# TensorE's parts of the S5 set-up behind later elementwise parts, small loads on GpSimd's queue, a first block split at 256 columns

## The chip, the core and the metric

The kernel runs on one core of one Trainium2 chip. The core's engines run side by side and each takes its own instructions strictly in the order in which they stand: TensorE (PE in the profile, its weight loads PEld), VectorE (DVE), ScalarE (ACT), GpSimd (POOL) and SyncE (SP), which here only starts DMA transfers. Sixteen DMA engines move the data. The metric is the device time of one launch in microseconds; lower is better.

## The reference

One layer of a hybrid decoder. 2064 prompt rows (16 meta tokens and 2048 tokens) and 8 running sequences of 4 tokens each pass through it, with a model width of 1024, all in float32:

```python
hn = rms_norm(x, lp['norm_mix_pre'])
proj = hn @ lp['w_in']                                  # 1024 x 4616
u, qkv, z, a, bt, gates = jnp.split(proj, [o1, o2, o3, o4, o5], axis=-1)
y_s5, h_re_n, h_im_n = s5_mix(u, ...)                   # 32 groups of a diagonal complex state, 64 states each
qkv_c, conv_new = short_conv(qkv, conv_buf, lp['gdn_conv_w'])      # 4 taps, then silu
g = -jnp.exp(gdn_A_log) * jax.nn.softplus(a + gdn_dt_bias)         # decay rates
beta = jax.nn.sigmoid(bt)
o, S = gdn_segment(q, k, v, g, beta, S)                 # gated delta rule, chunks of 64
mix = (sigmoid(ga) * br_a + sigmoid(gb) * br_b) @ lp['w_out']
x = x + rms_norm(mix, lp['norm_mix_post'])
x = x + rms_norm((silu(f @ w_ffn_gate) * (f @ w_ffn_up)) @ w_ffn_down, lp['norm_ffn_post'])
```

The S5 part needs tables that depend on the parameters alone: for each group the powers of a complex number `a_bar`, and matrices of 128 columns made of these powers with B and C.

## The kernel before, in words

The kernel works in phases: `p1` (the projection of the normalised input with `w_in`, the convolution, the S5 and the delta-rule work beside it), `merge`, `way_out`, `gate_up` and `down`. The change lies in `p1`, roughly the first 1300 of the 3287 us.

**The main stream.** A matrix product of float32 accuracy is three products of rounded parts (`mm3`, lines 161 to 163: high x high, high x low, low x high). The weight of 128 output columns (`wload`) comes by one DMA into `wr` (two buffers), is rounded by ACT into `wh`, and its remainder is split off in halves by POOL and DVE into `wl` (lines 146, 148, 149; three buffers each). The tokens come in blocks of 512 columns; block 0 has 560, since the 16 meta tokens and 32 sample tokens are with it. `p1_features` loads tiles of 128 tokens (`xt`, four buffers), squares them on ACT, makes the reciprocal root by a chain of a dozen small DVE operations, scales, transposes on PE (line 263), and writes `pgh` (ACT, line 268) and `pgl` (DVE, line 269). A pass takes two blocks with each unit of weights: 12 units of q, k, v (`psq`), 20 of gates (`psg`), 4 of u (`psu`). A product of more than 512 columns is cut in two by `colgroups`: 280 and 280.

**The side work.** After each half product of 8 k-steps `proj` calls `tick`, which advances four queues of generators by fractions of a step. `qf` holds the features of the next block, `qa` the delta rule's decays and triangular inverses, `qb` the S5 set-up and later the S5 groups, `qc` the delta-rule chunks. Each `yield` in a generator ends a step. `s5_setup` is such a generator; in its last part it handles the 32 groups in sets of four, and each set has five steps: V (POOL multiplies twice, DVE subtracts, line 1064, one DMA); K (PE multiplies V, line 1075, ACT copies, eight DMAs); V2 (line 1066); W (line 1062); and Wo (PE transposes W, line 1097, ACT copies, one DMA).

**What sets the order.** The instructions of an engine are not in the order of the code: the framework builds the whole program and then places each instruction by priority and by its own estimate of when operands are ready. So the order on each engine is fixed before the run, and an instruction that is late holds up all that stand behind it. Buffers come from pools: all of `ut`, `raw`, `cy`, `ct`, `gt`, V, V2, W and their helpers share one pool of eleven (`c2`).

**Small loads.** `gains` (lines 195 to 208) loads two gain vectors, the convolution's taps `cw` and the decay rates' constants `alog` and `dtb`, and computes `nea` from `alog` with `exp`, 15 small DVE operations. `pads` (338, 341) writes zeros to 20 places of two scratch tensors. All of them go by SP, as do the tokens and the weights.

Of the kernel before, what the change touches and what calls it, by code (L numbers as in the profile page):

```python
# [7 lines left out]
F32 = mybir.dt.float32  # L8
# [62 lines left out]
class Trunk:  # L71
# [118 lines left out]
    def gains(self):  # L190
        nc, c = self.nc, self.p1c
        def col(name, n):
            t = self.const.tile([P, n], F32, name="c_" + name)
            a = self.io[name]
            nc.sync.dma_start(t, ap_of(a, 0, [[1, P], [P, n]]))
            return t
# [4 lines left out]
        nc.sync.dma_start(self.cw, ap_of(self.io["gdn_conv_w"], 0, [[1, P], [1536, 4], [P, 12]]))  # L201
        self.alog = c.tile([P, H], F32, name="alog")
        nc.sync.dma_start(self.alog, ap_of(self.io["gdn_A_log"], 0, [[0, P], [1, H]]))
        self.dtb = c.tile([P, H], F32, name="dtb")
        nc.sync.dma_start(self.dtb, ap_of(self.io["gdn_dt_bias"], 0, [[0, P], [1, H]]))
        self.nea = c.tile([P, H], F32, name="nea")
        self.exp(self.nea, self.alog, "h")
        nc.vector.tensor_scalar(self.nea, self.nea, -1.0, None, op0=OP.mult)
# [103 lines left out]
    def p1_setup(self):  # L312
# [6 lines left out]
        for i in range(3):  # L319
            st = self.c2("stc")[:24, :512]  # L320
            nc.sync.dma_start(st, io["state_conv"].rearrange("o b j w -> (o b j) w")[:, 512 * i:512 * i + 512])
            sts.append(st)
# [10 lines left out]
    def pads(self):  # L333

        nc, z = self.nc, self.zero
        for m in range(4):
            for s, c in ((4, NL), (0, NL + 8)):
                nc.sync.dma_start(self.u_d[P * m:P * m + P, s:s + 4, c:c + 8],
                                  z[:, 0:32].rearrange("p (s n) -> p s n", s=4))
        for m in range(12):  # L340
            nc.sync.dma_start(ap_of(self.qkv_d, m * P * QW + NM, [[QW, P], [1, 16]]), z[:, 0:16])
# [4 lines left out]
    def p1_u(self, b, m, xh, xl, w):  # L346
# [5 lines left out]
        for c0, c1 in self.colgroups(width):  # L352
# [14 lines left out]
    def p1_qkv(self, b, m, xh, xl, w_):  # L367
# [10 lines left out]
        for c0, c1 in self.colgroups(width):  # L378
# [36 lines left out]
    def gdn_setup(self):  # L415
# [26 lines left out]
        nc.sync.dma_start(raw, self.wcols(self.w_in, C_AB, 8))  # L442
# [17 lines left out]
    def p1_ab(self, b, xh, xl):  # L460
# [3 lines left out]
        for c0, c1 in self.colgroups(width):  # L464
# [10 lines left out]
    def gdn_ab(self, b, ab):  # L475
# [43 lines left out]
        v.tensor_scalar(self.beta[:, sl], xa, 0.5, 0.5, op0=OP.mult, op1=OP.add)  # L519
        yield  # L520
# [363 lines left out]
    def s5_setup(self):  # L884
# [126 lines left out]
        for hf in range(2):  # L1011
# [37 lines left out]
            yield  # L1049
            for g0 in range(h0, h0 + 16, 4):  # L1050
# [20 lines left out]
                yield  # L1071

# [15 lines left out]
                V2 = f4(self.c2("V2"), 8)  # L1088
                outer(V2, (CR, CI), (R2, R1), "n", 1, 9)
                nc.sync.dma_start(self.wv_d[gs, :, 3].rearrange("g p (t c) -> p g t c", c=16), V2)  # L1090
                yield
                W = f4(self.c2("W"), 8)
                outer(W, (BR, BI), (W1, W2), "+", 0, 8)
                yield
                ps = self.pt.tile([P, BLK], F32, tag="pt", name="pst")
                for i in range(4):
                    nc.tensor.transpose(ps[:, P * i:P * i + P], W[:, i].rearrange("p t c -> p (t c)"), self.ident)
                Wo = self.tm.tile([P, D], F32, tag="tm", name="s5w").rearrange("p (g k m) -> p g k m", g=4, k=2)
                p4 = ps.rearrange("p (g m) -> p g m", g=4)
                nc.scalar.activation(Wo[:, :, 0], p4, AF.Copy)  # L1100
                nc.scalar.activation(Wo[:, :, 1, 0:64], p4[:, :, 64:P], AF.Copy)
                nc.scalar.activation(Wo[:, :, 1, 64:P], p4[:, :, 0:64], AF.Copy, scale=-1.0)
                nc.sync.dma_start(self.wv_d[gs, :, 0:2].rearrange("g p k m -> p g k m"), Wo)
                yield
# [105 lines left out]
    def p1_gate(self, b, m, xh, xl, w):  # L1210
# [5 lines left out]
        for c0, c1 in self.colgroups(width):  # L1216
# [731 lines left out]
```

## Time and profile before

| | us |
|---|---|
| median of 3 runs | 3285.52 (3281.97 to 3293.22) |
| the profiled execution | 3288.82 |
| its span in the profile | 3287.0 |
| PE busy in the span | 3105.4 (94%) |
| DVE busy in the span | 2015.5 (61%) |
| PE busy from 160 to 440 us | 249.34 of 280 |
| DVE busy from 160 to 440 us | 242.12 of 280 |

A row of the profile names the line of the kernel, the engine, the operation and the tile that it writes and reads. An engine with q behind its name (SPq) is its sequencer starting a DMA. The waits list says which engine waited for which line of another, how long in total, how often, and the longest time. PEclk is the share of its full clock that TensorE was granted.

### The profile page before, as it was taken

Reading aid. Unit: us, or ns where it says so; the run is one execution under the profiler, and the core shown is the slowest. Engines: PE = TensorE matmul, PEld = TensorE weight load, DVE = VectorE, ACT = ScalarE, POOL = GpSimd, SP = SyncE. Lnnn points to the kernel's source line nnn. Section 1 sums busy time; section 2 is a strip of 40 time slices with the busy share of each in tenths; the row PEclk is TensorE's granted clock in tenths of the full one; section 3 lists DMA queues with packets and bytes.
Section 4 is the critical chain, followed back from the end, with each engine's and each line's share of the span. In section 5 each row is a group of like instructions: output and inputs, shape, how many; then the busy total and the mean of one; then the engine's idle time right before and its main releaser. Section 6 shows DMA issues by size and latency. Waiting matters only on the chain. (4 is left out here: it accounts for less than half of the span.)

```text
span 3287.0 us, 47621 instructions
## 1 busy us (share of the span) xinstructions
PE 3105.4 (94%) x17461; PEld 2709.1 (82%) x17461; DVE 2015.5 (61%) x4648; ACT 1120.6 (34%) x1944; POOL 910.1 (28%) x903
## 2 busy tenths in 40 slices
PE   6998999999999999999999699999999999999998
PEld 5887778877777777988777699999999998887776
DVE  6888854657897546553444766676676664246235
ACT  4633222433232224221233444444444444223211
POOL 1123441123332212201111344434434444122110
PEclk9999999999999999999999799999999999999999
DMA  5336456545465435653553433333333334235224
GB/s 118 123 101 178 123 156 182 123 122 149 140 190 168 126 110 156 189 158 119 176 180 127 154 104 104 103 121 104 103 103 107 103 103 134 92 102 141 82 59 69
DMA packets 469018, 419.30 MB, mean 128 GB/s; under 512 B 120794, under 2 KB 393370, under 8 KB 468784
## 3 DMA queue, kind: packets, MB, share of 16 engines
q1 hardware_dynamic: 458576, 382.18, 39.9%
q0 software_dynamic: 10208, 34.09, 3.7%
q8 instruction: 137, 2.24, 0.3%
q14 instruction: 97, 0.79, 0.1%
HBM read 288.27 MB, written 127.65 MB: 127 GB/s over the span
## 5 line engine op out<-in xcount | busy, mean ns | idle before, releaser
L161 PE MATMUL psf<-xh,ah 128*128 128x348 f32 (+1 forms) x1848 | 598.8, 324 | 31.9 <-ACT sn L1534 20.2
L163 PE MATMUL psf<-xh,al 128*128 128x348 f32 (+1 forms) x1848 | 593.2, 321 | 6.8 <-DVE al L1476 6.8
L162 PE MATMUL psf<-xl,ah 128*128 128x348 f32 (+1 forms) x1848 | 593.0, 321 | 0.0
L161 PEld LDWEIGHTS psf<-xh,ah 128*128 128x128 f32 x1848 | 348.1, 188 | 41.5 <-ACT sn L1534 29.0
L163 PEld LDWEIGHTS psf<-xh,al 128*128 128x128 f32 x1848 | 347.6, 188 | 7.1 <-DVE al L1476 7.1
L162 PEld LDWEIGHTS psf<-xl,ah 128*128 128x128 f32 x1848 | 348.1, 188 | 0.0
L161 PE MATMUL psg<-pgh,wh 128*128 128x512 f32 (+1 forms) x800 | 300.0, 375 | 1.3 <-ACT wh L146 1.3
L1638 PE MATMUL psr<-wu,hh 128*128 128x512 f32 (+2 forms) x748 | 295.4, 395 | 4.2 <-POOL wu L148 4.2
L163 PE MATMUL psg<-pgh,wl 128*128 128x512 f32 (+1 forms) x800 | 291.4, 365 | 6.0 <-DVE wl L149 5.2
L1637 PE MATMUL psr<-wu,hh 128*128 128x512 f32 (+2 forms) x748 | 294.3, 395 | 0.0
L162 PE MATMUL psg<-pgl,wh 128*128 128x512 f32 (+1 forms) x800 | 291.3, 364 | 0.0
L1640 PE MATMUL psr<-wu,hl 128*128 128x512 f32 x704 | 277.6, 395 | 0.0
L148 POOL TENSOR_TENSOR wl<-wr,wh 128x512 fp32r<-128x512 f32 x92 | 143.8, 1563 | 389.5 <-ACT wh L146 318.9
L161 PE MATMUL psq<-pgh,wh 128*128 128x512 f32 (+1 forms) x480 | 180.4, 376 | 0.3 <-ACT pgh L268 0.3
L163 PEld LDWEIGHTS psg<-pgh,wl 128*128 128x128 f32 x800 | 155.5, 195 | 30.3 <-DVE wl L149 5.4
L1476 POOL TENSOR_TENSOR al<-R,ah 128x1024 fp32r<-128x1024 f32 x62 | 162.8, 2626 | 50.4 <-ACT ah L1475 50.4
L161 PEld LDWEIGHTS psg<-pgh,wh 128*128 128x128 f32 x800 | 156.0, 195 | 23.7 <-issue 2.9
L162 PEld LDWEIGHTS psg<-pgl,wh 128*128 128x128 f32 x800 | 155.9, 195 | 22.0 <-issue 2.5
L1638 PEld LDWEIGHTS psr<-wu,hh 128*128 128x128 f32 (+2 forms) x748 | 137.7, 184 | 42.9 <-POOL wu L148 6.7
L163 PE MATMUL psq<-pgh,wl 128*128 128x512 f32 (+1 forms) x480 | 172.9, 360 | 0.0
L162 PE MATMUL psq<-pgl,wh 128*128 128x512 f32 (+1 forms) x480 | 172.6, 360 | 0.0
L1637 PEld LDWEIGHTS psr<-wu,hh 128*128 128x128 f32 (+2 forms) x748 | 137.6, 184 | 35.9
(497 smaller groups left out, 6733.9 us busy)
## 6 DMA issues: line engine op xcount, KB each, us to landing
wr<-w_in SPq DMA_DIRECT2D x72, 512.0 KB
araw<-w_ffn_gate SPq DMA_DIRECT2D x31, 1024.0 KB
araw<-w_ffn_up SPq DMA_DIRECT2D x31, 1024.0 KB
wr<-w_ffn_down SPq DMA_DIRECT2D x44, 512.0 KB
zg_d<-gt SPq DMA_DIRECT2D x80, 256.0 KB
h_d<-hm SPq DMA_DIRECT2D x44, 348.0 KB
qkv_d<-cy SPq DMA_DIRECT2D x48, 256.0 KB
hr<-h_d SPq DMA_DIRECT2D x16, 768.0 KB
```

The costliest lines, as they stand in the source:

```text
L148: nc.gpsimd.tensor_sub(lo[:, :c], raw[:, :c], hi[:, :c].bitcast(F32))
L161: t.matmul(ps, wh, xh, start=first, stop=False, **kw)
L162: t.matmul(ps, wh, xl, start=False, stop=False, **kw)
L163: t.matmul(ps, wl, xh, start=False, stop=last, **kw)
L1476: eng.tensor_sub(flat(lo), x, flat(hi).bitcast(F32))
L1637: nc.tensor.matmul(ps, hi[:, k, cl], wh[:, cs], start=k == 0, stop=False)
L1638: nc.tensor.matmul(ps, hi[:, k, cl], wl[:, cs], start=False, stop=both and k == n - 1)
L1640: nc.tensor.matmul(ps, lo[:, k, c - c0:c - c0 + r], wh[:, cs], start=False, stop=k == n - 1)
```

## The change

- `gains`, `p1_setup`, `pads` and `gdn_setup` start their small loads and zero writes with `nc.gpsimd` and no longer with `nc.sync`.
- `alog`, `dtb` and `nea` move from `gains` to `gdn_setup`.
- `p1` cuts the 560 columns of block 0 at 256 (256 and 304) and no longer at 280; the other phases keep `colgroups`.
- `gdn_ab` has one more `yield` before the matmuls that sum up the decays.
- In `s5_setup` a set of four groups has four steps: V; V2; W; K. The transposes and copies of W (`late`) run at the start of the V2 step of the following set, and once more at the end of a half.

```diff
@@ gains
             a = self.io[name]
-            nc.sync.dma_start(t, ap_of(a, 0, [[1, P], [P, n]]))
+            nc.gpsimd.dma_start(t, ap_of(a, 0, [[1, P], [P, n]]))
             return t
         self.g_ffn = col("norm_ffn_pre", 8)
         self.g_gdn = col("gdn_norm", 1)
         nc.vector.tensor_scalar(self.g_gdn, self.g_gdn, 0.5, None, op0=OP.mult)
         self.cw = c.tile([P, 4, 12], F32, name="cw")
-        nc.sync.dma_start(self.cw, ap_of(self.io["gdn_conv_w"], 0, [[1, P], [1536, 4], [P, 12]]))
-        self.alog = c.tile([P, H], F32, name="alog")
-        nc.sync.dma_start(self.alog, ap_of(self.io["gdn_A_log"], 0, [[0, P], [1, H]]))
-        self.dtb = c.tile([P, H], F32, name="dtb")
-        nc.sync.dma_start(self.dtb, ap_of(self.io["gdn_dt_bias"], 0, [[0, P], [1, H]]))
-        self.nea = c.tile([P, H], F32, name="nea")
-        self.exp(self.nea, self.alog, "h")
-        nc.vector.tensor_scalar(self.nea, self.nea, -1.0, None, op0=OP.mult)
+        nc.gpsimd.dma_start(self.cw, ap_of(self.io["gdn_conv_w"], 0, [[1, P], [1536, 4], [P, 12]]))

@@ p1_setup
             st = self.c2("stc")[:24, :512]
-            nc.sync.dma_start(st, io["state_conv"].rearrange("o b j w -> (o b j) w")[:, 512 * i:512 * i + 512])
+            nc.gpsimd.dma_start(st, io["state_conv"].rearrange("o b j w -> (o b j) w")[:, 512 * i:512 * i + 512])
             sts.append(st)
@@ pads, p1_cols
             for s, c in ((4, NL), (0, NL + 8)):
-                nc.sync.dma_start(self.u_d[P * m:P * m + P, s:s + 4, c:c + 8],
+                nc.gpsimd.dma_start(self.u_d[P * m:P * m + P, s:s + 4, c:c + 8],
                                   z[:, 0:32].rearrange("p (s n) -> p s n", s=4))
         for m in range(12):
-            nc.sync.dma_start(ap_of(self.qkv_d, m * P * QW + NM, [[QW, P], [1, 16]]), z[:, 0:16])
+            nc.gpsimd.dma_start(ap_of(self.qkv_d, m * P * QW + NM, [[QW, P], [1, 16]]), z[:, 0:16])
+
+    def p1_cols(self, width):
+        return [(0, 256), (256, width)] if width > BLK else [(0, width)]

@@ p1_u
-        for c0, c1 in self.colgroups(width):
+        for c0, c1 in self.p1_cols(width):
             ps = self.pm.tile([P, BLK], F32, tag="pm", name="psu")[:, :c1 - c0]
@@ p1_qkv
-        for c0, c1 in self.colgroups(width):
+        for c0, c1 in self.p1_cols(width):
             ps = self.pm.tile([P, BLK], F32, tag="pm", name="psq")[:, :c1 - c0]
@@ gdn_setup
         self.abw = c.tile([P, 8, 2, 8], F32R, name="abw")
-        nc.sync.dma_start(raw, self.wcols(self.w_in, C_AB, 8))
+        nc.gpsimd.dma_start(raw, self.wcols(self.w_in, C_AB, 8))
+        self.alog = c.tile([P, H], F32, name="alog")
+        nc.gpsimd.dma_start(self.alog, ap_of(self.io["gdn_A_log"], 0, [[0, P], [1, H]]))
+        self.dtb = c.tile([P, H], F32, name="dtb")
+        nc.gpsimd.dma_start(self.dtb, ap_of(self.io["gdn_dt_bias"], 0, [[0, P], [1, H]]))
+        self.nea = c.tile([P, H], F32, name="nea")
+        self.exp(self.nea, self.alog, "h")
+        nc.vector.tensor_scalar(self.nea, self.nea, -1.0, None, op0=OP.mult)
         r = raw.rearrange("p a b -> p (a b)")
@@ gdn_ab
-        for c0, c1 in self.colgroups(width):
+        for c0, c1 in self.p1_cols(width):
             ps = self.pm.tile([P, BLK], F32, tag="pm", name="psa")[:16, :c1 - c0]
@@ gdn_ab
         v.tensor_scalar(self.beta[:, sl], xa, 0.5, 0.5, op0=OP.mult, op1=OP.add)
+        yield
         yield
@@ s5_setup
             yield
+            late = None
             for g0 in range(h0, h0 + 16, 4):
@@ s5_setup
                 yield
+                if late:
+                    late()
+                V2 = f4(self.c2("V2"), 8)
+                outer(V2, (CR, CI), (R2, R1), "n", 1, 9)
+                nc.sync.dma_start(self.wv_d[gs, :, 3].rearrange("g p (t c) -> p g t c", c=16), V2)
+                yield
+                W = f4(self.c2("W"), 8)
+                outer(W, (BR, BI), (W1, W2), "+", 0, 8)
+                yield

@@ s5_setup
                 yield
-                V2 = f4(self.c2("V2"), 8)
-                outer(V2, (CR, CI), (R2, R1), "n", 1, 9)
-                nc.sync.dma_start(self.wv_d[gs, :, 3].rearrange("g p (t c) -> p g t c", c=16), V2)
-                yield
-                W = f4(self.c2("W"), 8)
-                outer(W, (BR, BI), (W1, W2), "+", 0, 8)
-                yield
-                ps = self.pt.tile([P, BLK], F32, tag="pt", name="pst")
-                for i in range(4):
-                    nc.tensor.transpose(ps[:, P * i:P * i + P], W[:, i].rearrange("p t c -> p (t c)"), self.ident)
-                Wo = self.tm.tile([P, D], F32, tag="tm", name="s5w").rearrange("p (g k m) -> p g k m", g=4, k=2)
-                p4 = ps.rearrange("p (g m) -> p g m", g=4)
-                nc.scalar.activation(Wo[:, :, 0], p4, AF.Copy)
-                nc.scalar.activation(Wo[:, :, 1, 0:64], p4[:, :, 64:P], AF.Copy)
-                nc.scalar.activation(Wo[:, :, 1, 64:P], p4[:, :, 0:64], AF.Copy, scale=-1.0)
-                nc.sync.dma_start(self.wv_d[gs, :, 0:2].rearrange("g p k m -> p g k m"), Wo)
-                yield
+
+                def late(gs=gs, W=W):
+                    ps = self.pt.tile([P, BLK], F32, tag="pt", name="pst")
+                    for i in range(4):
+                        nc.tensor.transpose(ps[:, P * i:P * i + P], W[:, i].rearrange("p t c -> p (t c)"), self.ident)
+                    Wo = self.tm.tile([P, D], F32, tag="tm", name="s5w").rearrange("p (g k m) -> p g k m", g=4, k=2)
+                    p4 = ps.rearrange("p (g m) -> p g m", g=4)
+                    nc.scalar.activation(Wo[:, :, 0], p4, AF.Copy)
+                    nc.scalar.activation(Wo[:, :, 1, 0:64], p4[:, :, 64:P], AF.Copy)
+                    nc.scalar.activation(Wo[:, :, 1, 64:P], p4[:, :, 0:64], AF.Copy, scale=-1.0)
+                    nc.sync.dma_start(self.wv_d[gs, :, 0:2].rearrange("g p k m -> p g k m"), Wo)
+            yield
+            late()
+            yield

@@ p1_gate
-        for c0, c1 in self.colgroups(width):
+        for c0, c1 in self.p1_cols(width):
             ps = self.pm.tile([P, BLK], F32, tag="pm", name="psg")[:, :c1 - c0]
```

**GpSimd's queue at the start.** `c_norm_ffn_pre`, `c_gdn_norm`, `cw`, `abr`, `alog` and `dtb` are small loads; `u_d` and `qkv_d` are the scratch tensors that get zeros; a shape such as 128x48x1 means 48 single elements in each of 128 partitions. Before:

```order
L172 IOTA jp 128x128
L422 IOTA ii 64x64
L423 IOTA ip 64x1
L452 MEMSET U 128x512
L452 MEMSET T_756 64x256
L148 TENSOR_TENSOR wl<-wr,wh 128x512 x2
L1078 MEMSET s5k 16x4x128
```

After:

```order
L172 IOTA jp 128x128
L195 DMA c_norm_ffn_pre<-norm_ffn_pre 128x8x1
L195 DMA c_gdn_norm<-gdn_norm 128x1
L201 DMA cw<-gdn_conv_w 128x48x1
...
L438 DMA abr<-w_in 128x8x8
L440 DMA alog<-gdn_A_log 128x4
L148 TENSOR_TENSOR wl<-wr,wh 128x512
L442 DMA dtb<-gdn_dt_bias 128x4
...
L331 DMA u_d<-zero 128x4x8 x7
L148 TENSOR_TENSOR wl<-wr,wh 128x512
L331 DMA u_d<-zero 128x4x8
L334 DMA qkv_d<-zero 128x16 x12
L148 TENSOR_TENSOR wl<-wr,wh 128x512
```

The first, second and third POOL half of `wl` now stand behind 5, 13 and 26 DMAs; before, none stood there.

**SP's queue at the start**, the tokens `xt` and the weights `wr`. Before, from the third row of tokens on:

```order
L223 DMA xt<-x_prompt 128x1024 x2
L195 DMA c_norm_ffn_pre<-norm_ffn_pre 128x8x1
...
L144 DMA wr<-w_in 128x8x128
...
L223 DMA xt<-x_prompt 16x1024
L225 DMA xt<-x_sample 32x1024
L228 DMA xt<-x_prompt 128x1024
...
L228 DMA xt<-x_prompt 128x1024 x2
...
L228 DMA xt<-x_prompt 128x1024
...
L144 DMA wr<-w_in 128x8x128 x3
```

After:

```order
L216 DMA xt<-x_prompt 128x1024 x2
L144 DMA wr<-w_in 128x8x128 x3
L216 DMA xt<-x_prompt 16x1024
L218 DMA xt<-x_sample 32x1024
L221 DMA xt<-x_prompt 128x1024
L144 DMA wr<-w_in 128x8x128
L221 DMA xt<-x_prompt 128x1024 x3
```

The fifth weight load now stands ahead of three of block 1's four token tiles; with two buffers of `wr` it can start only when the third `wl` is split. Before, the third to fifth stood behind all the tokens.

**The S5 set-up on GpSimd**, from the first set's V on (`ow` is the second product of a pair). Before:

```order
L1059 TENSOR_TENSOR V<-s5c,s5r 128x576
L148 TENSOR_TENSOR wl<-wr,wh 128x512
L1060 TENSOR_TENSOR ow<-s5c,s5r 128x576
L1083 TENSOR_TENSOR s5k<-s5k,dg 16x4x16
L1059 TENSOR_TENSOR V_3038<-s5c,s5r 128x512
L1060 TENSOR_TENSOR ow<-s5c,s5r 128x512
L1081 TENSOR_TENSOR dg<-ident,s5a 16x64
L148 TENSOR_TENSOR wl<-wr,wh 128x512
L1059 TENSOR_TENSOR W<-s5bb,s5rr 128x512
```

After:

```order
L1064 TENSOR_TENSOR V<-s5c,s5r 128x576
L148 TENSOR_TENSOR wl<-wr,wh 128x512
L1065 TENSOR_TENSOR ow<-s5c,s5r 128x576
L1064 TENSOR_TENSOR V_2959<-s5c,s5r 128x512
L1065 TENSOR_TENSOR ow<-s5c,s5r 128x512
L148 TENSOR_TENSOR wl<-wr,wh 128x512
L1064 TENSOR_TENSOR W<-s5bb,s5rr 128x512
L1065 TENSOR_TENSOR ow<-s5bb,s5rr 128x512
L1097 TENSOR_TENSOR s5k<-s5k,dg 16x4x16
```

K's addition (`s5k`), which waits for PE and ACT, stood between V and V2 and now stands behind W.

## The prediction

> **What bounds the kernel now.** I read the page's busy shares first, then the slices, the windows of the stage that the change touches, and the list of waits in it.
>
> ```profile
> PE 3105.4 (94%) x17461; PEld 2709.1 (82%) x17461; DVE 2015.5 (61%) x4648; ACT 1120.6 (34%) x1944; POOL 910.1 (28%) x903
> PE   6998999999999999999999699999999999999998
> DVE  6888854657897546553444766676676664246235
> 160.00:440.00 280.00, 249.34 (x1471) 220.83 (x1470) 242.12 (x852) 89.40 (x164) 102.62 (x118) 0.93 0.48 133
> 267.00:270.40 3.40, 3.40 (x11) 2.83 (x12) 2.95 (x18) 1.15 (x3) 0.00 (x0) 0.50 0.66 180
> 852.00:862.00 10.00, 7.28 (x27) 5.45 (x26) 8.93 (x43) 3.39 (x7) 0.63 (x2) 0.83 0.39 115
> ```
>
> In a row of the windows stand the stretch, its length, then PE, PEld, DVE, ACT and POOL busy, the granted clock, the DMA share and GB/s. TensorE bounds the whole (94%), so a microsecond is won only where TensorE stands still or runs slowly. The S5 set-up lies in 160 to 440 us, where TensorE idles 280 − 249.3 = 30.7 us and was granted 0.93 of its clock: 280 × 0.07 = 19.6 us more. The clock falls behind a standstill: TensorE waited 4.75 us before 266.9, and the next 3.4 us went at 0.50. But VectorE is busy for 242.1 of these 280 us: it is the next bound there, 37.9 us behind. TensorE's waits, for 160 to 440 us and in the last row for the whole run (total, times, longest):
>
> ```profile
> PE pst L1097 <- DVE W L1062: 12.5, 3, 4.8
> PE psg L163 <- DVE wl L149: 5.2, 1, 5.2
> PE pst L1075 <- DVE V L1064: 4.7, 1, 4.7
> PE pst L525 <- DVE k_gg L517: 3.2, 2, 1.9
> PE pst L1047 <- DMA ctl<-s_C_re: 3.0, 1, 3.0
> ...
> PE pst L525 <- DVE k_gg L517: 5.9, 3, 2.7
> ```
>
> **Part 1: W and V later on TensorE, one more step before the decays' sums.** One of the three waits for W, as the timeline of all engines has it:
>
> ```profile
> 260.83 2.31 DVE L395 SCALAR_TENSOR_TENSOR cy<-raw,cw,cy 128x512 f32<-128x512 f32 x3
> 263.27 1.11 POOL L1059 TENSOR_TENSOR W<-s5bb,s5rr 128x512 f32<-128x512 f32 x1 [3.46 <-DVE cy L395]
> 266.14 0.69 DVE L1062 TENSOR_TENSOR W<-W,ow 128x512 f32<-128x512 f32 x1
> 266.89 1.08 PE L1097 MATMUL pst<-ident,W 128*128 128x128 f32 x4 [4.75 <-DVE W L1062]
> ```
>
> POOL stood for 3.46 us until VectorE was through with the convolution, so W came late, and TensorE with its whole stream behind the four transposes. In the new order 24 products and four transposes more stand between W's first product and its transposes. How much time is that? The distance between two products comes from their starts:
>
> ```profile
> 119.83 0.29 PE L161 MATMUL psq<-pgh,wh 128*128 128x280 f32 x1
> ...
> 123.21 0.29 PE L163 MATMUL psq<-pgh,wl 128*128 128x280 f32 x1
> 123.62 0.40 PE L162 MATMUL psq<-pgl,wh 128*128 128x512 f32 x1
> ...
> 128.73 0.40 PE L163 MATMUL psq<-pgh,wl 128*128 128x512 f32 x1
> 46.31 0.60 PE L263 MATMUL pst<-ident,xt 128*128 128x128 f32 x4
> ```
>
> 3.38 us over 26 steps is 0.130 us for 280 columns; 5.11 over 22 is 0.232 for 512; a transpose takes about 0.11 (0.60 for four, less the pipeline's tail). So W's transposes stand 12 × 0.232 + 12 × 0.120 + 4 × 0.11 = 4.7 us later, about the longest wait (4.8), and W's POOL part moves up by one weight half. K's product of V comes two steps later still. The sums that need `k_gg` move by 23 × 0.232 = 5.3 us against a longest wait of 2.7. All three kinds can vanish: 12.5 + 4.7 + 3.2 = 20.4 of the 30.7 us in this stage. Their share of the lost clock is 20.4/30.7 × 19.6 = 13.0, so 33.4 us if nothing else becomes late.
>
> Something else does become late, since VectorE cannot do its 242.1 us in less. Its own waits there:
>
> ```profile
> DVE V L1064 <- POOL ow L1060: 14.6, 3, 5.8
> DVE wl L149 <- ACT wh L146: 5.8, 6, 2.8
> ```
>
> Of its 37.9 idle us the 14.6 for POOL's product of V are not touched: V, `ow` and a weight half stand on POOL in the same succession as before. That leaves 37.9 − 14.6 = 23.3 as the most that the stage can shrink. TensorE's wait of 5.2 for `wl` is one for VectorE too, and a stage that runs faster brings it nearer: the late thing after W and V is `wl`. I leave it standing and take 23.3 − 5.2 = **−18**, between 0 (VectorE hands every microsecond over to `wl`) and −23.3. V and W also hold their buffers of the pool of eleven a step or two longer; the price is inside these ends.
>
> The third wait for `k_gg` lies at 853 us, outside the stage: 2.7 us and 10 × 0.17 = 1.7 of clock. VectorE is busy for 8.93 of the 10 us there, so of 4.4 I take **−2** (0 to −4.4).
>
> **Part 2: small loads by GpSimd.** No row shows such loads on POOL, so their price is bounded from POOL's other DMAs (mean ns of one behind the busy time):
>
> ```profile
> L287 POOL DMA_DIRECT2D f_d<-fo x36 | 26.0, 722 | 165.9 <-ACT fo L286 161.5 <-issue 4.3
> L1405 POOL DMA_DIRECT2D y_prompt<-xr x16 | 8.9, 554 | 11.1 <-DVE xr L1404 11.1
> L1654 POOL DMA_DIRECT2D y_prompt<-facc x16 | 13.8, 859 | 79.5 <-DVE facc L1651 79.5
> ```
>
> One of 128 rows takes 0.554 us, one with two pieces in each partition (256) 0.722: 0.55 each, and 0.168 for every further 128 pieces. By this `c_norm` (8 x 128 pieces) takes 1.7, `c_gdn` 0.55, `cw` (48 x 128) 8.4: 11.8 with the 1.1 us of constants ahead. `abr` (8 x 128) and `alog` make 14.1, and the first weight half (1.27) ends at 15.4. Then `dtb`, seven `u_d` of 4 x 128 (1.05 each) and the second half: 24.6; one `u_d`, twelve `qkv_d` and the third half: 33.5.
>
> What waits for that is SP. The fourth weight load needs the second half, and the last 48 tokens of block 0 stand behind it; the fifth needs the third, and three tiles of block 1 stand behind it. Before, they went like this (SP), and TensorE's starts answer to them:
>
> ```profile
> 8.72 5.65 SPq L203 DMA_DIRECT2D alog<-gdn_A_log  x1
> ...
> 19.85 0.44 SPq L223 DMA_DIRECT2D xt<-x_prompt  x1
> ...
> 28.51 0.84 SPq L228 DMA_DIRECT2D xt<-x_prompt  x2
> ...
> 36.45 0.33 SPq L228 DMA_DIRECT2D xt<-x_prompt  x1
> 10.64 1.27 POOL L148 TENSOR_TENSOR wl<-wr,wh 128x512 fp32r<-128x512 f32 x1 [8.63 <-ACT wh L146]
> 24.59 0.60 PE L161 MATMUL psq<-pgh,wh 128*128 128x280 f32 x1
> 52.74 2.11 PE L263 MATMUL pst<-ident,xt 128*128 128x128 f32 x8 [5.58 <-DVE xt L252]
> ```
>
> SP loses the 5.65 us for which `alog` was stuck behind `cw`, and products of 256 columns need only the first two token tiles, so the first product can come before 24.59. But it lacks the tail at once: the 48 tokens go out at 24.6 and not at 19.85 (4.7 later), block 1's second tile at 34 and not at 28.5 (5.5 later), its last one earlier than 36.45. TensorE's total work here is the same, so what counts is when block 1 can run on. I take **+3**, between 0 and 5.5, since the last tile gains. Its ends: −5.6 if each DMA costs 0.55 whatever its pieces (1.1 + 26 × 0.55 + 3 × 1.27: the third half can be through at 19, and the 5.58 us wait ahead of 52.74 goes). If instead each further 128 pieces cost a whole DMA (0.55), the 85 further ones ahead of the third half cost 85 × (0.554 − 0.168) = 32.8 us more: +36. The row of 859 ns is between: 26 × 0.305 = 7.9 more, +11.
>
> A rule of the Trainium skill bears on these ends: DMA: Bandwidth & Descriptors, "Anatomy of one DMA — SWDGE (gpsimd) path", says that many descriptors can be emitted before their number is felt; by it the start gains 5.6, while the rows above show a step of 0.168 at 256 pieces already. Against the change speaks SBUF — State Buffer, "SBUF: two separate sides": a DMA of GpSimd's queue cannot have its descriptors written while VectorE runs in a mode that takes both ports. The 859 beside 554 ns for the same shape would fit; by it the start is +11.
>
> **Part 3: 256 and 304.** 0.232/512 × 560 columns is 0.254, and twice 0.130 is 0.260: the two halves cost by column, so the cut is free. Bound: if 256 costs no less than 280, 36 units x 24 products x 0.0106 us = +9.2.
>
> **The sum** on the profiled execution's 3288.8 us (span 3287.0): −18 − 2 + 3 = −17, so 3271.8. That execution lies 3.3 above the median of 3285.5, so **3269** on the median. Between 440 and 500 us, behind the stage, what is won is kept, since TensorE does not wait at all:
>
> ```profile
> 440.00:500.00 60.00, 60.00 (x358) 48.41 (x357) 25.33 (x59) 11.99 (x30) 22.76 (x25) 0.94 0.64 177
> ```
>
> **Rivals.** (a) Slower: POOL's DMAs go by pieces. One place decides, the three weight halves behind `cw` (48 x 128 pieces), `abr` and the zeros on POOL. If a further 128 pieces cost 0.55 us, the start is +36 against −20 in the two other terms: 3285.5 + 16 = 3301.5. It turns to a loss from 85 × (p − 0.168) = 17, that is p = 0.37 us. For it: pieces of 4 bytes have no row here. Against it: the step of 0.168 is less than half of that. Chance 0.17. (b) The same: VectorE takes the waits over. The transposes no longer wait, but `wl`, 242.1 of 280 us busy as VectorE is, arrives as late as W did; parts 1 and 2 leave 0 and +3: 3288.5. For it: the wait of 5.2 for `wl` is already there. Against it: 23.3 idle us. Chance 0.20. (c) All of it works: −23.3 − 4.4 − 5.6 = −33.3, so 3252; it needs `wl` on time in a fuller stage. Chance 0.13. That the moves aren't made at all is excluded by the new order, where they stand.
>
> **Numbers.** The forecast has 0.50, by itself from 3258 (−23.3 − 4.4 + 0) to 3283 (start +11, the third `k_gg` wait left, and the stage at −14, where a second wait for `wl` comes, as long as W's mean, 12.5/3 = 4.2). A measurement can tell 0.3% (9.9 us) from no change: faster is below 3275.7, slower above 3295.4. Of the forecast 0.42 lies below and 0.08 within; with (c) faster has 0.55, with (b) the same has 0.28 less 0.01, and (a) with that 0.01 makes slower 0.18. The range, 3249 to 3298, leaves out most of (a).
>
> **What would show it.** Right: the waits for W, V and `k_gg` are gone from TensorE's list, the granted clock in the stage rises above 0.93 and VectorE's share there towards 0.93. Wrong by (b): the idle time stands there under `wl`. For the start the timeline of POOL gives `cw`'s time (8.4 us is the sum's, 0.55 the flat price, 26 rival (a)'s) and where the third weight half ends (33.5), and SP's the time of block 1's second tile (34). If the wait before block 1's second token pair grows beyond 5.58 by more than 17 us, the prediction is wrong in its sign.

## The result and the profile after

The changed kernel takes 3310.48 us (median of 9 runs), the kernel before 3294.09 on the same chips. The ratio is 1.0057, 95% interval 1.0042 to 1.0072: slower by 18.7 us (14 to 24), where 17 us of gain were forecast. The profiled execution has a span of 3303.8 us.

TensorE's waits between 160 and 440 us in the changed kernel (total, times, longest):

```profile
PE psk L597 <- DMA kTa<-qkv_d: 10.5, 3, 8.5
PE pst L1051 <- DMA ctl<-s_C_re: 5.3, 1, 5.3
PE pst L1106 <- DVE bt L637: 5.2, 1, 5.2
PE psq L161 <- ACT gt L1230: 2.1, 1, 2.1
PE psg L161 <- ACT raw L378: 1.2, 1, 1.2
PE psg L161 <- ACT gt L1230: 0.7, 1, 0.7
```

The waits for V and `k_gg` are gone, of the three for W one is left (now put down to `bt`, which VectorE does just before). In their place stand `kTa`, the keys that the delta rule loads for its decays, and three waits for ACT, which clears the results of the main stream into `gt` and `raw` (evictions), together 14.5 us. The wait for `ctl`, a load for the set-up, grew from 3.0 to 5.3. The windows of the changed kernel, by stage:

```profile
0.00:60.00 60.00, 29.29 (x172) 26.03 (x172) 39.66 (x161) 29.99 (x65) 26.44 (x42) 0.91 0.54 125
160.00:440.00 280.00, 254.92 (x1533) 226.14 (x1533) 241.89 (x827) 93.59 (x177) 112.79 (x130) 0.95 0.48 135
440.00:800.00 360.00, 344.76 (x2295) 287.51 (x2294) 199.17 (x585) 114.87 (x281) 67.92 (x111) 0.95 0.53 138
1290.00:1345.00 55.00, 37.80 (x268) 35.34 (x269) 36.33 (x89) 22.20 (x44) 14.21 (x15) 0.75 0.61 175
```

and of the kernel before, for the stages that the prediction does not show:

```profile
0.00:60.00 60.00, 34.70 (x191) 29.86 (x192) 41.69 (x170) 32.71 (x71) 6.19 (x13) 0.94 0.62 134
440.00:800.00 360.00, 350.44 (x2367) 293.19 (x2366) 196.52 (x564) 120.90 (x292) 85.81 (x127) 0.98 0.55 144
1290.00:1345.00 55.00, 44.27 (x353) 41.45 (x352) 40.32 (x96) 22.84 (x47) 13.44 (x13) 0.91 0.74 215
```

In the stage of the set-up TensorE idles 25.1 us where it was 30.7, at 0.95 of its clock where it was 0.93. Little of that can be credited to the change: a second profile of the kernel before, shown below, has 29.0 us and 0.95 there. Around the stage TensorE loses. In the first 60 us it does 5.4 us less; from 440 to 800 us it does 5.7 less at a lower clock, and behind 1290 6.5 less at 0.75 of the clock. These stretches do not hold the same work in both kernels: the main stream of the first phase ends at 1294.2 us before and at 1281.0 in the changed kernel, which has more of the delta rule left then.

### The profile page after: what moved, and what is told of

It reads as the page before. It is cut to its first block, busy times and chain, and to the rows that moved or that the text cites. A ratio compares the mean times of both kernels' runs of the same rounds, so it can differ in the third digit from the quotient of the medians.

```text
span 3303.8 us, 47641 instructions
## 1 busy us (share of the span) xinstructions
PE 3118.0 (94%) x17461; PEld 2722.4 (82%) x17461; DVE 2024.7 (61%) x4648; ACT 1120.2 (34%) x1946; POOL 925.6 (28%) x932
## 5 line engine op out<-in xcount | busy, mean ns | idle before, releaser
L161 PE MATMUL psg<-pgh,wh 128*128 128x512 f32 (+2 forms) x800 | 299.5, 374 | 1.9 <-ACT raw L378 1.2
L163 PE MATMUL psg<-pgh,wl 128*128 128x512 f32 (+2 forms) x800 | 289.7, 362 | 3.3 <-DVE wl L149 3.3
L162 PE MATMUL psg<-pgl,wh 128*128 128x512 f32 (+2 forms) x800 | 288.3, 360 | 0.0
L161 PE MATMUL psq<-pgh,wh 128*128 128x512 f32 (+2 forms) x480 | 182.2, 379 | 4.6 <-ACT pgh L261 2.2
L162 PE MATMUL psq<-pgl,wh 128*128 128x512 f32 (+2 forms) x480 | 174.6, 364 | 0.5 <-DVE pgl L262 0.5
L163 PE MATMUL psq<-pgh,wl 128*128 128x512 f32 (+2 forms) x480 | 174.4, 363 | 0.0
```

What stands on the lines that cost most here:

```text
L161: t.matmul(ps, wh, xh, start=first, stop=False, **kw)
L162: t.matmul(ps, wh, xl, start=False, stop=False, **kw)
L163: t.matmul(ps, wl, xh, start=False, stop=last, **kw)
```

## The experiments

All ratios are against the kernel before, run on the same chip (6 to 12 runs of each version); the microseconds are the ratio less one, times 3291.

| run | ratio | interval | us |
|---|---|---|---|
| changed kernel | 1.0057 | 1.0042 to 1.0072 | +18.7 |
| set-up's order alone | 1.0017 | 1.0005 to 1.0029 | +5.6 |
| step in gdn_ab alone | 1.0024 | 1.0014 to 1.0034 | +7.9 |
| loads by GpSimd alone | 1.0030 | 1.0017 to 1.0043 | +9.9 |
| cut at 256 alone | 1.0018 | 1.0005 to 1.0031 | +5.9 |
| changed, old set-up | 1.0045 | 1.0031 to 1.0058 | +14.8 |
| changed, no step | 1.0062 | 1.0046 to 1.0078 | +20.4 |
| changed, cut at 280 | 1.0067 | 1.0050 to 1.0084 | +22.0 |
| changed, zeros by SP | 1.0064 | 1.0041 to 1.0087 | +21.1 |

**The parts, each alone.** The set-up's order is the new `s5_setup` in the kernel before; the other edits are single pieces of the diff.

> The kernel before with the new order of the S5 set-up alone. Theory A (the start pays: what the set-up wins is kept, and the small loads on GpSimd's queue lose more): faster by 8 to 15 us, and TensorE's waits for W and V in 160 to 440 us gone. Theory B (the delta rule's chain of chunks sets the end of the first phase, and the new order of the side work makes it later): no faster, within 5 us of before or slower, the first transposes of o (pT) later than 512 us and the idle time of TensorE after 1290 us more than the 9 us of before.

> The kernel before with the one more step in gdn_ab alone. Theory A: within 4 us of before, the waits for k_gg (5.9 us) gone. Theory B: everything behind that step in its queue comes about one step (5 to 8 us) later, the products psk from 213 us on and with them the chunks; slower by 5 to 10 us, the loss lying after 1290 us.

> The kernel before with the small loads and zero writes on GpSimd's queue and the decay rates' constants later, without the cut at 256. Theory A: slower by 10 to 17 us, the same work of TensorE 5 us or more later from 60 us on. Theory B: 0 to 5 us later from 60 us on, and no more than that at the end (0 to +5).

> The kernel before with block 0 cut at 256 and 304 alone. Both theories: within 5 us of before. The first product comes before 24.6 us, since it needs two token tiles and not three; theory A has the rest of the start unchanged, since the tokens of block 0's tail go out as late as before (19.9 us).

Every part is slower by itself, and their sum, 29.3, is more than the whole. Theory A falls for the set-up, which was to win 8 to 15 us. It is no faster, as theory B has it, but not for B's reason: the first `pT` does come later, at 517.8 us (before: 512.3), yet between 1290 and 1345 us TensorE idles 10.2 us, where before it was 10.7. The step alone does what it was made for, the waits for `k_gg` are gone, but the wait for V grows from 4.7 to 10.5 us. The loads lose 9.9 us, just under theory A's 10 to 17, and block 1's second token pair is met 5.2 us later. The cut brings the first product to 16.3 us instead of 24.6, as expected, and is slower all the same. What took the waits' place with the set-up's order alone is shown by that run's waits, 160 to 440 us:

```profile
PE psk L593 <- DMA kTa<-qkv_d: 9.6, 3, 7.9
PE psg L161 <- ACT raw L382: 7.7, 2, 6.3
PE psq L161 <- ACT gt L1226: 5.2, 2, 3.5
PE pst L525 <- DVE k_gg L517: 3.2, 2, 1.8
```

Before, W, V and `wl` made 12.5 + 4.7 + 5.2 = 22.4 us. They are all but gone, and `kTa` and ACT's evictions into `raw` and `gt` make 22.5. The idle time is 32.6 us (before: 30.7). The timeline of this run says why `kTa` is late:

```profile
308.06 1.13 DVE L609 SCALAR_TENSOR_TENSOR Z<-Z,rb,mlo 128x128 f32<-128x128 f32 x4
309.22 0.34 SPq L610 DMA_DIRECT2D m_d<-Z  x1
311.24 0.53 SPq L587 DMA_DIRECT2D kTa<-qkv_d  x1
```

SP starts nothing from 302.5 to 309.2 us: it holds the store of Z, which VectorE finishes at 309.2, and the load stands behind that store. VectorE's lateness reaches TensorE through SP. It reaches it through ACT too, whose own waits in this stretch name the set-up:

```profile
ACT gt L1226 <- DVE V L1067: 12.8, 2, 8.0
ACT gt L1226 <- DVE W L1063: 9.9, 1, 9.9
```

The eviction into `gt` reads neither V nor W, but all three take their buffers from the pool of eleven. In the changed kernel these waits make 21.9 us; in the kernel before there is none in one profile and one of 5.2 us in the other. That a buffer held longer by the new order is what `gt` waits for follows from the code and these rows; a larger pool was not tried.

**The set-up: another queue for `kTa`, and less work for VectorE.**

```diff
-            nc.sync.dma_start(kT, ap_of(self.qkv_d, 512 * QW + c0, [[QW, P], [P * QW, H], [1, nt]]))
+            nc.gpsimd.dma_start(kT, ap_of(self.qkv_d, 512 * QW + c0, [[QW, P], [P * QW, H], [1, nt]]))
```

> The kernel before with the new order of the S5 set-up, and the loads kTa issued by GpSimd and not by SP. Theory K (the wait of 9.6 us for kTa, most of what the new order of the set-up lost, comes from SP: the load stands behind the store of Z, which waits for VectorE): the wait for kTa is below 3 us, and the kernel is 6 to 10 us faster than with the new order alone, so 3284 to 3289 where before is 3292. Rival D (VectorE is the bound in 160 to 440 us, and hands the time on to another wait): within 4 us of the new order alone, with other waits of TensorE for VectorE or ACT in the place of the one for kTa.

The ratio is 1.0037 (1.0023 to 1.0051), +12.2 us: not faster than the order alone, where theory K has 6 to 10 us (the two intervals overlap). The wait for `kTa` falls from 9.6 to 4.2 us, not below 3, and others grow by as much, as rival D has it: ACT's two from 12.9 to 14.6, those for `wl` and `ctl` by about 2 us each (160 to 440 us):

```profile
PE psq L161 <- ACT gt L1226: 10.4, 5, 3.3
PE psg L161 <- ACT raw L382: 4.2, 1, 4.2
PE psk L593 <- DMA kTa<-qkv_d: 4.2, 1, 4.2
...
160.00:440.00 280.00, 247.49 (x1441) 217.74 (x1439) 243.57 (x847) 86.46 (x162) 112.85 (x131) 0.93 0.47 131
```

TensorE idles 32.5 us, as much as with the order alone.

Then half of VectorE's work on the triangular inverses was left out, with the old order and with the new one:

```diff
         for j in range(1, 31):
             r = 31 - j
+            if j % 2:
+                continue
```

> The kernel before without half of VectorE's work on the triangular inverses (the steps with odd j are left out; some 27 us of VectorE between 160 and 440 us, as much again in the second half). By itself the base of the next run. Theory D (VectorE's load is what makes its operands late in 160 to 440 us): TensorE's waits there shrink, 5 to 15 us faster than before. Rival P (the waits come from the order alone): within 4 us of before.

> The same work left out, with the new order of the S5 set-up. Theory D: with VectorE relieved the new order wins what it was made for, 8 us or more faster than the run with the old order and the same work left out. Rival P: within 5 us of it or slower (with all of VectorE's work the new order was 5.6 us slower).

With the old order this is 0.9946 (0.9931 to 0.9961) of before, 17.8 us faster; with the new order 0.9981 (0.9967 to 0.9995), 6.3 us faster. VectorE's work is worth time here, as theory D says, but with VectorE relieved of some 20 of its 242 us in the stage the new order is 11.5 us behind the old one. The windows (old order, then new) show it in the stage itself; ahead of the first stands TensorE's longest wait there with the old order:

```profile
PE pst L1099 <- DVE W L1064: 12.2, 3, 4.6
...
160.00:440.00 280.00, 255.19 (x1542) 226.60 (x1541) 218.31 (x795) 91.22 (x167) 107.67 (x127) 0.96 0.50 141
```

```profile
160.00:440.00 280.00, 249.54 (x1491) 220.40 (x1490) 222.15 (x794) 87.92 (x166) 116.64 (x130) 0.95 0.47 134
```

TensorE idles 24.8 us with the old order and 30.5 with the new; in the new one `kTa` alone costs 12.2. The waits for W, the largest kind, are as long as before (12.5) though VectorE has 62 idle us and not 38: they come from the order, as rival P says, and not from how much VectorE has to do. Nor is the new order waiting for a less busy VectorE: theory D falls in this part. The same the other way round, the changed kernel with the old set-up:

> The changed kernel with the old order of the S5 set-up. If the parts add up (alone: set-up +5.6, step +7.9, loads +9.9, cut +5.9; together +18.7 and not +29.3), the rest is 10 to 18 us above before. Theory D (the set-up's new order only moves TensorE's waits): within 6 us of the changed kernel, the waits for W and V back with about 17 us and the one for kTa gone.

1.0045: 3.9 us less than the changed kernel. The intervals overlap, so inside it the order wins nothing that shows, and may cost as much as alone. The waits for W and V are back with 21 us, that for `kTa` is down to 0.6.

**The start.** Three runs separate the small loads, the taps and the zeros. The changed kernel's timeline of POOL, then of SP:

```profile
3.09 2.26 POOL L201 DMA_DIRECT2D cw<-gdn_conv_w  x1
14.00 1.76 POOL L148 TENSOR_TENSOR wl<-wr,wh 128x512 fp32r<-128x512 f32 x1 [7.00 <-ACT wh L146]
16.99 5.42 POOL L331 DMA_DIRECT2D u_d<-zero  x7
24.42 4.37 POOL L334 DMA_DIRECT2D qkv_d<-zero  x8
31.74 1.28 POOL L148 TENSOR_TENSOR wl<-wr,wh 128x512 fp32r<-128x512 f32 x1
```

```profile
5.18 19.59 SPq L144 DMA_DIRECT2D wr<-w_in  x3
27.92 0.33 SPq L216 DMA_DIRECT2D xt<-x_prompt  x1
33.05 0.38 SPq L144 DMA_DIRECT2D wr<-w_in  x1
33.96 10.12 SPq L221 DMA_DIRECT2D xt<-x_prompt  x3
```

The first run keeps `cw` with SP and moves the rest; the second keeps the zeros of `pads` with SP; the third is the changed kernel with the zeros back on SP.

```diff
@@ pads
-                nc.gpsimd.dma_start(self.u_d[P * m:P * m + P, s:s + 4, c:c + 8],
+                nc.sync.dma_start(self.u_d[P * m:P * m + P, s:s + 4, c:c + 8],
...
-            nc.gpsimd.dma_start(ap_of(self.qkv_d, m * P * QW + NM, [[QW, P], [1, 16]]), z[:, 0:16])
+            nc.sync.dma_start(ap_of(self.qkv_d, m * P * QW + NM, [[QW, P], [1, 16]]), z[:, 0:16])
```

> The kernel before with the small loads and zero writes on GpSimd's queue, but the convolution's taps cw (6144 pieces of 4 bytes) still on SP's. Theory C (the pieces of cw hold up the tokens and the first weights in the DMA engines, by which the first transposes are at 17.6 and not at 14.0 us): the first transposes at 14 to 15 us and the same work of TensorE no more than 2 us later than before from 60 us on. Rival O (the weights that now stand ahead of the tokens on SP's queue and wait for the halves of wl make the start late): 3 to 5 us later from 60 us on, as with all small loads on GpSimd.

> The kernel before with the small loads on GpSimd's queue, but the 20 writes of zeros still on SP's; by that SP has block 1's second and third tile ahead of the third weight load again. Theory O (late is what SP holds: weight loads stand ahead of the tokens and wait for halves of wl, which stand behind the zero writes on POOL): the wait before block 1's second token pair is back at 53 to 54 us, and the same work of TensorE no more than 1.5 us later than before from 60 us on. Rival C (cw's small pieces hold up the DMA engines): 3 to 5 us later from 60 us on, as with everything on GpSimd (4.5).

> The changed kernel with the 20 writes of zeros back on SP's queue. Theory O (they hold up the halves of wl on POOL, by these the weight loads on SP, and by these the tokens): the same work of TensorE no more than 2 us later than before at 60 us (changed: 5.3), and 4 to 10 us faster than the changed kernel, so 3299 to 3305 where before is 3290. Rival N (any new order costs some us, the changed kernel's loss has no place): within 3 us of the changed kernel.

With `cw` on SP: 1.0045 (1.0030 to 1.0060), no better than with everything on GpSimd (1.0030). With the zeros on SP: 1.0002 (0.9985 to 1.0019), the whole 9.9 us are back. So it is the zeros. On POOL they stand ahead of the second and third half of `wl`; by these SP's weight loads wait, and the tokens behind them. With the zeros back on SP, SP also has its third weight load behind block 1's second and third tile again, and TensorE meets block 1's second token pair at 54.6 us (theory O: 53 to 54; before: 52.7). Which of the two counts, the halves or SP's order, no run separates. Inside the changed kernel theory O doesn't hold: with the zeros on SP it is as slow as with them on POOL, and its timeline of SP shows the 20 writes between the tokens:

```profile
5.64 14.53 SPq L331 DMA_DIRECT2D u_d<-zero  x8
26.58 0.33 SPq L216 DMA_DIRECT2D xt<-x_prompt  x1
32.37 0.81 SPq L221 DMA_DIRECT2D xt<-x_prompt  x2
42.58 0.34 SPq L221 DMA_DIRECT2D xt<-x_prompt  x1
```

Block 1's last tile is issued at 42.6 us (before: 36.45), and TensorE meets block 1's second token pair at 57.8 us, where the changed kernel had 58.5. Yet the kernel before with the zeros on SP has the same writes between its tokens and the last tile at 41.2 us, and is level with before; SP's queue doesn't explain the 21 us either.

**The step in gdn_ab.** More steps in its queue make the decays late, and the order of the program shows one more chunk of the delta rule behind the last product of the main stream. So the step was taken out of the changed kernel; put in with a higher rate of the chunks; and put in for blocks 0 and 1, or 2 and 3, alone.

```diff
-        self.rates = (3.0, 0.5, 0.65, 0.75, 1.0, 1.4)
+        self.rates = (3.0, 0.5, 0.65, 0.75, 1.0, 1.5)
...
+        if b < 2:
+            yield
```

> The changed kernel without the one more step in gdn_ab. Theory T (the step delays the delta rule's decays, so that one more of its chunks is left when the main stream of the first phase ends, and is worked off with nothing beside it): the idle time of TensorE after 1290 us falls back to before's 9 us, and some 13 to 16 us of the 18.7 that the change lost come back; 3294 to 3301 where before is 3292. Rival N (the step costs nothing; any new order costs some us somewhere): within 5 us of the changed kernel.

> The kernel before with the one more step, and with the rate of the chunks raised from 1.4 to 1.5 steps per product of 512 columns, so that as many chunks as before are left when the main stream ends. Theory T: the step alone was 10 us ahead at 1290 us and lost 16 after it; with the rate the loss after 1290 us is gone, and the kernel is faster than before by 5 to 10 us. Rival N: slower than before by 3 to 10 us, as the step alone.

> The kernel before with the one more step in gdn_ab for blocks 0 and 1 alone. Theory T (the step loses only by the steps of blocks 2 and 3, which leave one more chunk for the end): as many chunks as before are left at the end, two of the three waits for k_gg are gone, and it is 0 to 8 us faster than before. Rival N (any new order costs): 4 us or more slower.

> The kernel before with the one more step for blocks 2 and 3 alone. Theory T: one more chunk is left for the end, idle time and half clock after 1290 us grow by 12 to 16 us, of which some comes back earlier: slower by 8 to 13 us. Rival N: within 4 us of the run with the step for blocks 0 and 1.

Without the step the changed kernel is at 1.0062: nothing comes back, though only one chunk is left at the end and the idle time from 1290 to 1345 us is down to 8.9. With the step and the rate: 1.0012 (1.0001 to 1.0022), +3.9, not faster. With the step for blocks 0 and 1: 1.0024 (1.0011 to 1.0038), the whole +7.9, and no chunk more at the end. With that for blocks 2 and 3: 1.0005 (0.9990 to 1.0020), nothing, although its end shows the loss most clearly:

```profile
1290.00:1345.00 55.00, 38.75 (x257) 36.43 (x256) 36.69 (x85) 21.72 (x43) 12.67 (x12) 0.72 0.60 176
```

TensorE does 5.5 us less there than before, at 0.72 of the clock. But from 800 to 1290 us it does more, since the chunk did not have to be done there:

```profile
800.00:1290.00 490.00, 471.34 (x2606) 381.85 (x2605) 342.38 (x1104) 152.04 (x313) 131.28 (x237) 0.99 0.54 151
```

471.3 us against before's 465.2. Theory T falls: the loss at the end is work put off, and repaid in advance. What the step for the first blocks costs lies between 440 and 800 us, where TensorE is busy for 343.9 us and not 350.4 (348.3 in the second profile of before); no single wait there grows by more than 2.2 us, so no wait explains it.

**The cut.**

> The changed kernel with block 0 cut at 280 again. Theory S (the cut costs by itself, as alone, +5.9): 4 to 8 us faster than the changed kernel. Rival N (the cut moves the order by chance, alone to the worse): within 4 us of the changed kernel or slower.

With the cut at 280 the changed kernel is at 1.0067, +22.0: not faster. Alone the cut costs 5.9 us, inside the changed kernel it costs nothing or wins 3. Theory S falls.

**Both kernels once more.** The same two programs were profiled a second time.

> The kernel before, profiled once more. Both theories expect the same waits of TensorE in 160 to 440 us (22 us for W, V and wl), and no difference beyond 10 us of span; it shows which part of the differences between profiles comes without any edit, above all the stretch at half clock around the products pSs at 490 us.

> The changed kernel, profiled once more. TensorE's idle time in the first phase is the same within 3 us (84), kTa's wait included (10.5). If the lost clock is chance, it moves by up to 10 us, as between the two profiles of before (37 and 49); if it belongs to the changed order, it stays at 54 or more.

The spans are 3295.9 us (before: 3287.0 the first time) and 3295.4 (changed: 3303.8 the first time). The main waits are the same ones: `kTa` 11.1 us in the changed kernel, W 12.7 in the kernel before. The smaller ones are not: before's wait for `wl` is 0.7 us and not 5.2, its wait for V 7.2 and not 4.7. The windows of the second profile of before, then of the changed kernel:

```profile
0.00:60.00 60.00, 34.27 (x193) 28.45 (x194) 42.09 (x170) 33.20 (x72) 6.19 (x13) 0.91 0.61 134
160.00:440.00 280.00, 250.97 (x1492) 221.75 (x1492) 243.38 (x855) 89.49 (x165) 102.71 (x121) 0.95 0.48 133
440.00:800.00 360.00, 348.31 (x2322) 290.53 (x2321) 192.79 (x548) 118.43 (x287) 82.99 (x121) 0.96 0.54 142
1290.00:1345.00 55.00, 44.61 (x307) 40.91 (x307) 38.00 (x88) 24.93 (x51) 14.81 (x12) 0.81 0.64 186
```

```profile
0.00:60.00 60.00, 29.03 (x175) 25.01 (x176) 40.51 (x163) 30.65 (x67) 26.33 (x42) 0.91 0.53 125
160.00:440.00 280.00, 253.70 (x1531) 225.43 (x1530) 243.10 (x827) 92.78 (x172) 112.92 (x130) 0.95 0.48 136
440.00:800.00 360.00, 346.45 (x2305) 287.47 (x2304) 202.75 (x592) 117.05 (x284) 71.92 (x113) 0.96 0.53 141
1290.00:1345.00 55.00, 36.83 (x283) 34.79 (x283) 39.45 (x92) 22.36 (x44) 13.38 (x15) 0.78 0.66 192
```

What repeats is the busy time: 5.4 and 5.2 us less in the first 60 us, 2.7 to 5.6 more in the set-up's stage, 6.5 and 7.8 less at the end (from 440 to 800 us it is 5.7 and 1.9). What doesn't repeat is the clock: before lost 360 × 0.02 = 7 us between 440 and 800 in one execution and 14 in the other, 5 and 10 us behind 1290. So the 16.8 us between the first two profiles cannot be put down to places: about half of it comes and goes without an edit. The idle time is steadier. Over the whole span TensorE idles 181.6 and 180.7 us before, 185.8 and 189.0 in the changed kernel. Up to the delta rule's last transposes `pT`, by which both kernels have done the same work, it is 99.6 and 99.3 against 101.6 and 103.7. So 4 to 8 us of the loss are idle time, and none of the 18 that the stage was to win is there.

**The clock of all runs.** Every run also has TensorE's mean granted clock over its span on record. In 111 runs of the kernel before it lies between 0.973 and 0.982, with a mean of 0.9780, and by a straight line through them each 0.001 less goes with 2.7 us more: the mean time is 3279.2 us at 0.982 (three runs), 3292.0 at 0.978 (17) and 3304.6 at 0.973 (one). The nine runs of the changed kernel lie between 0.971 and 0.975. The fourth column is an estimate from these numbers: the difference of the clocks at 2.7 us for 0.001:

| version | mean clock | before, same chip | us by the clock | us measured |
|---|---|---|---|---|
| changed kernel | 0.9726 | 0.9780 (all chips) | +14.5 | +18.7 |
| set-up's order alone | 0.9788 | 0.9779 | −2 | +5.6 |
| step in gdn_ab alone | 0.9751 | 0.9779 | +8 | +7.9 |
| loads by GpSimd alone | 0.9768 | 0.9779 | +3 | +9.9 |
| cut at 256 alone | 0.9742 | 0.9779 | +10 | +5.9 |

So most of the changed kernel's loss goes with a lower clock, and so does all that the step and the cut lose. The loss of the set-up's order and most of the loads' lie elsewhere. Why some of these orders are granted less clock no run shows.

## Why the prediction was wrong, by its steps

- **"What bounds the kernel": right.** TensorE bounds the whole, VectorE is next in the stage. VectorE is busy for 241.9 of 280 us after the change, 242.1 before.
- **"All three kinds can vanish": right for the waits.** 20.4 us of them became 5.2 (one for W), and the third wait for `k_gg`, outside the stage, is gone too. The share of the lost clock that was to come back with them, 13.0 us, did not: over the whole span the changed kernel is granted 0.9726 and not 0.9780, and the sum had no term for that, an estimated 14.5 of the 18.7 us.
- **"I leave it standing and take −18": the step that failed.** I counted a wait as won when its instruction moved away, and let VectorE's 23.3 idle us be the room. The runs show the waits exchanged: 22.4 us for W, V and `wl` against 22.5 for `kTa` and ACT with the set-up's order alone, 30.7 idle us against 32.6. Late next was not `wl`, as I had it, but what else hangs on VectorE's chain: SP, held by the store of Z, and ACT's evictions, held by V and W. For that last I had a sentence, that V and W hold their buffers of the pool longer, and gave it no price of its own; ACT's waits for them are 22.7 us with the set-up's order alone. With `kTa` on another queue other waits grew by as much. VectorE's idle us were not the room either: with 62 of them in place of 38 the waits for W stayed at 12.2 us. The term measured +5.6 alone (1.6 to 9.5), and the step in gdn_ab +7.9 alone, where both together were to win 20 with the third `k_gg` wait.
- **Part 2, "+3 for the start": just beyond its upper end, the way to it half right.** TensorE meets block 1's second token pair at 58.5 us for 52.7, 5.7 later, against an upper end of 5.5. Block 1's second tile went out at 33.96 us, for 34 in the sum, and the third half of `wl` ended at 33.0 for 33.5. The price per piece was wrong: `cw` took 2.26 us and not 8.4, that is 0.036 us for each further 128 pieces and not 0.168. That the end agreed is chance: the first half waited for ACT's `wh` until 14.0, since the first weights came late. Alone the loads cost 9.9 us, some 3 of them by the clock estimate; what they cost beyond the later start was not in the sum.
- **Part 3, "the cut is free": open.** It is +5.9 alone and −3 inside the changed kernel (the intervals overlap); alone the lower clock more than makes up the loss, so the work itself may be free, as the sum has it.
- **Rival (a), slower by POOL's DMAs: the place was right (the halves of `wl` behind the zeros), the mechanism wrong.** It needed pieces at 0.37 us for 128.
- **Rival (b), VectorE takes the waits over, was nearest in kind**, with `kTa` and ACT in the place of `wl`. It had 0 for parts 1 and 2 beside the start; the measured kernel lies some 16 us above that, outside the range.
- **The two pages.** DMA: Bandwidth & Descriptors of the Trainium skill ("Anatomy of one DMA — SWDGE (gpsimd) path") says that many descriptors can be emitted before their number is felt. By `cw`'s 0.036 us for 128 pieces the trace is nearer to it than to my price. SBUF — State Buffer of the Trainium skill ("SBUF: two separate sides") says that a DMA of GpSimd's queue can't have its descriptors written while VectorE runs in a mode that takes both ports. The `u_d` writes of the changed kernel took 0.77 us each (5.42 for seven), below the 1.05 of the sum, so no hold-up shows in them; in which mode VectorE ran just then no view says. The row of 859 ns that I held against the change need not be a sign of it: in the code (line 1654) that DMA also adds to what it writes to, and the one of 554 ns (line 1405) doesn't.

What stays open: why four parts that cost 29.3 us alone cost 18.7 together, and what lowers the granted clock in the changed kernel, the step and the cut. Of the moves tried none was clearly faster than before while it did the same work; two were level (the zeros on SP, the step for blocks 2 and 3). No version beat the kernel before.

## What to carry to other kernels

- A wait that one takes from an in-order engine by moving the waiting instruction is only won when the next thing that hangs on the late engine is on time; list everything that the late engine feeds (here by SP's stores and by buffers that ACT's evictions need too) and sum the engine's idle time, not the wait that was aimed at.
- Compare the idle time and the clock of two profiles apart, and profile one of them twice: here the clock alone moved the span by 9 us without an edit. Where every run has its granted clock on record, compare that too: it placed most of a loss that the profiles could not.

## What the runs showed of the hardware

**The clock falls without a standstill.** Around the 16 products `pSs` (32 of 128 rows, 512 columns) TensorE is busy without a gap and yet at half its clock. The second profile of before, and the cut alone:

```profile
484.00:498.00 14.00, 14.00 (x41) 8.38 (x40) 8.96 (x30) 1.92 (x9) 1.99 (x1) 0.62 0.64 179
```

```profile
498.00:512.00 14.00, 14.00 (x36) 8.57 (x35) 6.41 (x23) 0.48 (x2) 0.00 (x0) 0.50 0.80 211
```

How long this lasts changes from one execution to the next with the same program: 6.8 us in the first profile of before and 17.1 in the second, 20.5 with the cut alone. That the few rows are its cause was not tried.

**A load of small pieces beside large ones.** In the changed kernel `cw` goes out beside the first weights and tokens. From 10 to 14 us the DMA engines' busy share is 0.99 to 1.00, and they move less than a third of what the kernel before reached at 8 to 10 us; the changed kernel's windows, then before's:

```profile
10.00:12.00 2.00, 0.00 (x0) 0.00 (x0) 1.57 (x15) 0.00 (x0) 0.00 (x0) 1.00 0.99 95
12.00:14.00 2.00, 0.00 (x0) 0.00 (x0) 0.05 (x1) 1.06 (x1) 0.00 (x0) 1.00 1.00 113
```

```profile
8.00:10.00 2.00, 0.00 (x0) 0.00 (x0) 0.94 (x10) 1.46 (x3) 0.00 (x0) 1.00 1.09 376
```

The first weights reach ACT at 12.86 us and not at 9.50, and the first transposes start at 17.67 and not at 14.03. That it is `cw` is shown by the run with `cw` on SP: there the engines move 407 GB/s from 10 to 12 us, and the first transposes start at 15.21. Yet it meets block 1's second token pair at 60.9 us, later than ever.
